# Tanh for sigmoid, Newton steps on GpSimd and a shared key length in the RWKV stage of a macaron block

## The chip, the core and the metric

The kernel runs on one core of a Trainium2 chip. The metric is the device time of one execution in microseconds. A core has engines that work side by side, each through its own queue in order: TensorE (PE; its weight loads are shown as PEld), VectorE (DVE), ScalarE (ACT), GpSimd (POOL), and SyncE (SP), which issues the transfers. Semaphores tie them together: the instruction at a queue's head waits until its inputs and its output buffer are ready, and everything behind it in that queue waits too.

## The reference

Two layers, 512 tokens, 1024 channels, float32 throughout. Each layer is a half feed-forward, a mixing layer and another half feed-forward. The mixing layer joins RWKV-7, gated linear attention and attention over 256 memory rows, each weighted by a sigmoid gate per channel. What the change touches, for 8 RWKV heads of width 64:

```python
v = v + (v_first - v) * jax.nn.sigmoid(v0 + (v @ v1) @ v2)          # second layer only
w_log = -jax.nn.softplus(-(w0 + jnp.tanh(wl) @ w2)) - 0.5           # decay = exp(-exp(w_log))
a = jax.nn.sigmoid(a0 + al @ a2)
kk = kk / jnp.maximum(jnp.linalg.norm(kk, axis=-1, keepdims=True), 1e-12)
k_h = heads(k) * (1.0 + (a_h - 1.0) * k_a)
# per token: state = state * w_t + sa (kk_t * a_t)^T + v_t k_t^T;  y_t = state r_t
yn = (y - mean) * lax.rsqrt(var + RWKV_LN_EPS) * ln_w + ln_b
...
gates = jax.nn.sigmoid(u_gate.reshape(b, s, N_BRANCH, d))
merged = jnp.einsum('bsjc,jcd,bsjd->bsd', branches, w_branch[l], gates)
```

The decay only needs exp(-0.5) * sigmoid(w0 + tanh(wl) w2), so it is a sigmoid too.

## The kernel before

Activations lie with channels on the 128 partitions and 512 tokens along the free axis. Every large product is done three times over, with each float32 operand split into a high part (whi, xhi; L171, an ACT copy) and a low part (wlo, xlo; L172, a DVE subtraction). The weight halves have three buffers each, so ACT and DVE must keep up with TensorE all the time. Line 286 is such a product inside the mixing layer, lines 187 to 189 elsewhere.

The RWKV part is cut into 8 blocks per layer: 4 pairs of heads (hp) times 2 halves of the sequence (hf, 256 tokens, four chunks of 64). A block passes through four generators: `rwkv_gates` (decay, a, the normalized key kk; L359), `rwkv_first` (scaled keys, the chunks' matrices A and Z, the transposed keys KBT), `rwkv_inverse` (inverts the chunk matrices by doubling blocks; X is a 32x32-block transpose of Z by DVE, L510) and `rwkv_second` (the recurrence over chunks; L569 reads the state S, L570 makes qs, L575 applies the inverse, L576 and L577 copy the result into VU, L581 and L587 update S). At its end stands the tail: the product L597, the sums L602 to L607, the square L609 and its sum L611, the deviation L612 to L614, then the transposes L620 on TensorE. Sigmoids for the gates of the branches are in `gate_g`, their use in `branch_g`. Attention heads (L776 to L799) run beside it.

The function `weave` orders TensorE's work by hand. It keeps a clock of planned nanoseconds: each generator yields the TensorE time of its step and how long ACT and DVE will need before its next step, such as

```python
yield 5 * 218, 8500
```

for the tail, to which 400 are added. While no step is due, the order is filled with matmuls of the other branches and projections (L286), one at a time. TensorE's queue keeps exactly this order; if a step's inputs are later than planned, TensorE waits there and all the filling behind it waits too. The order on the other engines comes from a scheduler that places instructions by priority, the block's before the filling's.

ACT evaluates its functions from a table. Where the next function is not in the table that is loaded, an ACT_TABLE_LOAD stands ahead of it in ACT's queue. In the weave Sigmoid, Exp and Sqrt follow each other, in the order the blocks happen to be in.

## Time and profile before

| | us |
|---|---|
| three runs | 2820.02, 2819.43, 2811.11 |
| their median | 2819.43 |
| the profiled execution | 2812.78 |
| its span, first to last instruction | 2811.0 |
| idle time of TensorE, 584 to 940 us (weave, first layer) | 28.2 of 356.0 |
| the same, 1973 to 2332 us (second layer) | 24.3 of 359.0 |
| idle time of TensorE, 1000 to 1795 us (feed-forward) | 0.3 of 795.0 |

A group's row gives the line, the engine, the operation, output and inputs, their shapes, the count, then busy time in us and the mean of one in ns, then the engine's idle time ahead of these instructions and what ended it. A wait's row gives who waited, for whom, and us in total, times and the longest. A matmul's duration (0.39 us for 128x512) includes its way through the array; in a full queue such matmuls follow each other every 0.23 us.

### The profile page before, as it was taken

To read this page: it belongs to the slowest core of one execution; us is meant where nothing else is said; L and a number is where in the kernel's file an instruction comes from. 1 tells how busy PE (TensorE), PEld (TensorE's weight loads), DVE (VectorE), ACT (ScalarE), POOL (GpSimd) and SP (SyncE) were. 2 spreads that over 40 slices of the span, in tenths; PEclk is the share of its full clock that TensorE was granted. 3 is DMA by queue.
4 is the path that set the end of the run, shared out by engine and by line. 5 is a ranking of instruction groups with operands and counts; after the bars stand their busy time and mean duration, and the time that the engine had idled before them with its cause. 6 is when DMAs were issued, how large, how long until landed. Compare 5 with 4: busy or idle time off the path is not lost.

```text
span 2811.0 us, 35290 instructions
## 1 busy us (share of the span) xinstructions
PE 2724.6 (97%) x13296; PEld 2231.9 (79%) x13296; DVE 1636.1 (58%) x3069; ACT 1233.3 (44%) x2097; POOL 21.3 (1%) x118
## 2 busy tenths in 40 slices
PE   8999999998999999999999999999999899999998
PEld 6888887777777888888888888877777788888886
DVE  6434446777877655444454344567788776543444
ACT  5323345665554443333343233465655544432332
POOL 0000000000000000000000000000000000000000
PEclk9999999999999999999999999999999999999999
DMA  5232332211111332222332223312111113322222
GB/s 184 96 100 98 101 135 73 98 58 53 59 64 49 107 118 98 92 103 93 102 105 94 101 98 113 129 68 90 59 59 59 64 63 103 119 98 88 103 93 85
DMA packets 91722, 258.04 MB, mean 92 GB/s; under 512 B 10464, under 2 KB 24832, under 8 KB 91552
## 3 DMA queue, kind: packets, MB, share of 16 engines
q1 hardware_dynamic: 91552, 255.79, 26.5%
q8 instruction: 104, 1.70, 0.2%
q14 instruction: 66, 0.54, 0.1%
HBM read 243.69 MB, written 12.06 MB: 91 GB/s over the span
## 4 chain that ended last, share of the span: by engine, by line
PE 87%; DVE 6%; ACT 5%; issue 1%; DMA 0%; SPq 0%; DVEq 0%; ACTq 0%
PE ps_b L286 20%; PE ps_b L187 19%; PE ps_b L189 19%; PE ps_b L188 19%; PE ps_c L517 2%; PE ps_c L525 1%; PE ps_i L433 1%; DVE t L383 1%; PE ps_f L581 1%; ACT whi L171 1%; ACT L380 1%; PE ps_f L575 0%; PE ps_f L776 0%; PE ps_y L569 0%; PE ps_f L798 0%
## 5 line engine op out<-in xcount | busy, mean ns | idle before, releaser
L171 ACT ACTIVATE whi<-wraw 128x512 fp32r<-128x512 f32 (+1 forms) x874 | 543.3, 622 | 1136.3 <-PE ps_b L188 893.0
L172 DVE TENSOR_TENSOR wlo<-wraw,whi 128x512 fp32r<-128x512 f32 (+1 forms) x874 | 589.2, 676 | 478.0 <-ACT whi L171 474.5
L187 PE MATMUL ps_b<-xhi,whi 128*128 128x512 f32 x1424 | 555.9, 390 | 10.1 <-ACT xhi L197 8.2
L189 PE MATMUL ps_b<-xhi,wlo 128*128 128x512 f32 x1424 | 555.8, 390 | 0.5 <-DVE wlo L172 0.5
L188 PE MATMUL ps_b<-xlo,whi 128*128 128x512 f32 x1424 | 555.8, 390 | 0.0
L286 PE MATMUL ps_b<-xhi,whi 128*128 128x512 f32 x864 | 353.2, 409 | 7.6 <-ACT whi L171 5.8
L286 PE MATMUL ps_b<-xhi,wlo 128*128 128x512 f32 x864 | 350.6, 406 | 3.3 <-DVE wlo L172 3.2
L286 PE MATMUL ps_b<-xlo,whi 128*128 128x512 f32 x864 | 348.7, 404 | 0.0
L187 PEld LDWEIGHTS ps_b<-xhi,whi 128*128 128x128 f32 x1424 | 266.6, 187 | 66.9 <-ACT xhi L197 8.2
L189 PEld LDWEIGHTS ps_b<-xhi,wlo 128*128 128x128 f32 x1424 | 266.6, 187 | 58.1 <-DVE wlo L172 0.9
L188 PEld LDWEIGHTS ps_b<-xlo,whi 128*128 128x128 f32 x1424 | 266.4, 187 | 57.6 <-DVE xlo L198 0.8
L187 PE MATMUL ps_b<-mhi,whi 128*128 128x512 f32 x704 | 277.5, 394 | 0.0
L189 PE MATMUL ps_b<-mhi,wlo 128*128 128x512 f32 x704 | 276.0, 392 | 0.0
L188 PE MATMUL ps_b<-mlo,whi 128*128 128x512 f32 x704 | 273.3, 388 | 0.0
L286 PEld LDWEIGHTS ps_b<-xhi,whi 128*128 128x128 f32 x864 | 164.1, 190 | 45.0 <-ACT whi L171 7.9
L286 PEld LDWEIGHTS ps_b<-xhi,wlo 128*128 128x128 f32 x864 | 163.6, 189 | 39.4 <-DVE wlo L172 6.6
L286 PEld LDWEIGHTS ps_b<-xlo,whi 128*128 128x128 f32 x864 | 164.2, 190 | 30.8 <-issue 1.8
L189 PEld LDWEIGHTS ps_b<-mhi,wlo 128*128 128x128 f32 x704 | 132.1, 188 | 30.9
L188 PEld LDWEIGHTS ps_b<-mlo,whi 128*128 128x128 f32 x704 | 132.2, 188 | 29.5
L187 PEld LDWEIGHTS ps_b<-mhi,whi 128*128 128x128 f32 x704 | 132.4, 188 | 26.3
L262 DVE TENSOR_TENSOR fm<-ps_b,ft 128x512 f32<-128x512 f32 x88 | 60.8, 691 | 127.6 <-PE ps_b L189 127.6
L258 DVE TENSOR_TENSOR ft<-ps_b,rs 128x512 f32<-128x512 f32 x88 | 60.9, 692 | 126.0 <-PE ps_b L189 125.8
(298 smaller groups left out, 3362.9 us busy)
## 6 DMA issues: line engine op xcount, KB each, us to landing
wraw<-in_ffn_in_dram SPq DMA_DIRECT2D x176, 512.0 KB, 3.4
wraw<-in_w_main_dram SPq DMA_DIRECT2D x108, 512.0 KB, 3.4
wraw<-in_ffn_out_dram SPq DMA_DIRECT2D x64, 512.0 KB, 3.4
wraw<-in_ffn_out_dram SPq DMA_DIRECT2D x64, 192.0 KB, 2.3
wraw<-in_w_branch_dram SPq DMA_DIRECT2D x48, 256.0 KB, 2.5
wraw<-in_w_out_dram SPq DMA_DIRECT2D x16, 512.0 KB, 3.4
xd<-x SPq DMA_DIRECT2D x16, 256.0 KB, 2.1
wraw<-in_w_k_dram SPq DMA_DIRECT2D x8, 512.0 KB, 3.6
```

The source lines that it names most:

```text
L171: nc.scalar.activation(hi, r, AF.Copy)
L172: nc.vector.tensor_tensor(lo, r, hi.bitcast(F32), ALU.subtract)
L187: nc.tensor.matmul(ps, a[0], b[0], start=start, stop=False)
L188: nc.tensor.matmul(ps, a[0], b[1], start=False, stop=False)
L189: nc.tensor.matmul(ps, a[1], b[0], start=False, stop=stop)
L258: nc.vector.tensor_tensor(t, pp[0], rs, ALU.mult)
L262: nc.vector.tensor_tensor(m, pp[1], t, ALU.mult)
L286: self.nc.tensor.matmul(ps, w[k][a], xs[k][b], start=k + i == 0, stop=k == n - 1 and i == 2)
L380: nc.scalar.activation(nrm, psn, AF.Sqrt)
L383: nc.vector.reciprocal(rn, nrm)
L433: nc.tensor.matmul(pss[j][:, c * P:(c + 1) * P], KBc[js, c, :], AR[js, c, :], start=True, stop=True)
L517: nc.tensor.matmul(ps[:, u, :], AB[:, u, :], X[:, u, :], start=True, stop=True)
```

## The change

Sigmoids in the weave become tanh: sigmoid(z) is 0.5 tanh(z/2) + 0.5. The halved biases are made once per layer (`half`). For the decay the 0.5 and the sum are one more DVE instruction; elsewhere they go into an instruction that is there already, and the factor two that the branches carry is taken out when the sum is split (scale 0.5). The root of the deviation and its reciprocal become an integer first guess and three Newton steps on GpSimd, 14 dependent instructions on 128x4 values. The key's scaling, square, product with `blk` and root are done once for 512 tokens in a pair's first half. The reciprocal is cut into two of 128 columns. Z's sum with the identity moves ahead, the product KH behind the first steps of the inverse. The copies L539 and L576 go from DVE to ACT. The planner's entry for the tail falls from 8500 to 7500, and those of the gates change with their matmuls.

```diff
+    def hcol(self, name, i):
+        o = (16 if name == "v0" else COLS[name] - COLS["w0"]) + i
+        return self.half[:, o:o + 1]
...
@@ layer_params
+        self.half = self.const.tile([P, 20], F32, name="half", tag="half")
+        for o, name, n in ((0, "w0", 16), (16, "v0", 4)):
+            nc.vector.tensor_scalar(self.half[:, o:o + n], self.par[:, COLS[name]:COLS[name] + n], 0.5, None, ALU.mult)
...
@@ rwkv_rkv
-            nc.scalar.activation(sg, ps, AF.Sigmoid, bias=self.pcol("v0", hp))
+            nc.scalar.activation(sg, ps, AF.Tanh, bias=self.hcol("v0", hp), scale=0.5)
             nc.vector.tensor_tensor(vf, vf, v, ALU.subtract)
-            nc.vector.tensor_tensor(vf, vf, sg, ALU.mult)
-            nc.vector.tensor_tensor(v, v, vf, ALU.add)
+            nc.vector.scalar_tensor_tensor(vf, sg, 1.0, vf, ALU.add, ALU.mult)
+            nc.vector.scalar_tensor_tensor(v, vf, 0.5, v, ALU.mult, ALU.add)
@@ rwkv_gates
-        r, k, v = r[:, cs], k[:, cs], v[:, cs]
-        kk = t1("kk")
-        nc.scalar.activation(kk, k, AF.Copy, scale=self.pcol("k_k", hp))
-        sq = t1("t0", 2)
-        nc.scalar.activation(sq, kk, AF.Square)
-        yield 0, 1300
-
+        if hf == 0:
+
+            self.kk = self.rw.tile([P, T], F32, name="kk", tag="kk", bufs=1)
+            nc.scalar.activation(self.kk, k, AF.Copy, scale=self.pcol("k_k", hp))
+            sq, self.nrm_k = (self.lr.tile([P, T + 1], F32, name=n, tag="ush", bufs=2)[:, :T] for n in ("ksq", "knrm"))
+            nc.scalar.activation(sq, self.kk, AF.Square)
+            yield 0, 1800
+            psn = self.small("i")
+            nc.tensor.matmul(psn, self.c("blk"), sq, start=True, stop=True)
         psw = self.small("i")
...
-        psn = self.small("i")[:, :N]
-        nc.tensor.matmul(psn, self.c("blk"), sq, start=True, stop=True)
         sg, a = t1("sg"), t1("a")
-        nc.scalar.activation(sg, psw[:, :N], AF.Sigmoid, bias=self.pcol("w0", hp))
-        nc.scalar.activation(a, psw[:, N:], AF.Sigmoid, bias=self.pcol("a0", hp))
+        nc.scalar.activation(sg, psw[:, :N], AF.Tanh, bias=self.hcol("w0", hp), scale=0.5)
+        nc.scalar.activation(a, psw[:, N:], AF.Tanh, bias=self.hcol("a0", hp), scale=0.5)
+        if hf == 0:
+            nc.scalar.activation(self.nrm_k, psn, AF.Sqrt)
+        nc.vector.tensor_scalar(sg, sg, 0.5, 0.5, ALU.mult, ALU.add)
         G = t1("G")
         nc.vector.tensor_tensor_scan(G, self.c("reset")[:, :N], sg, 0.0, ALU.mult, ALU.add)
-        nrm = t1("t0", 2)
-        nc.scalar.activation(nrm, psn, AF.Sqrt)
+        r, k, v, kk, nrm = r[:, cs], k[:, cs], v[:, cs], self.kk[:, cs], self.nrm_k[:, cs]
+        kh = t1("t0")
+        nc.vector.tensor_scalar(kh, a, -1.0, self.hcol("k_a", hp), ALU.add, ALU.mult)
+        nc.vector.scalar_tensor_tensor(kh, kh, 1.0, k, ALU.add, ALU.mult)
         nc.vector.tensor_scalar(nrm, nrm, 1e-12, None, ALU.max)
-        rn = t1("t1", 2)
-        nc.vector.reciprocal(rn, nrm)
-        nc.vector.tensor_tensor(kk, kk, rn, ALU.mult)
...
-        nc.vector.tensor_tensor(a, kk, a, ALU.mult)
-        yield 3 * 432, 6500
+        for q in range(2):
+            nc.vector.reciprocal(nrm[:, q * P:(q + 1) * P], nrm[:, q * P:(q + 1) * P])
+        nc.vector.tensor_tensor(kk, kk, nrm, ALU.mult)
+        nc.vector.scalar_tensor_tensor(a, a, 1.0, kk, ALU.add, ALU.mult)
+        yield (2 * 432 if hf else 4 * 432), 6500
@@ rwkv_first
...
-        rk = self.t256("t1", 2)
+        nc.vector.tensor_tensor(Z, A4, self.c("eye").unsqueeze(1).to_broadcast([P, 4, 64]), ALU.add)
+        rk = t1("t1", 2)
         nc.vector.scalar_tensor_tensor(rk, r, self.pcol("r_k", hp), kh, ALU.mult, ALU.mult)
-        KH = rw.tile([P, 4, P], F32, name="KH", tag="KH", bufs=1)
-        nc.vector.tensor_tensor(KH, KBc, E[:, :, 64:65].to_broadcast([P, 4, P]), ALU.mult)
...
-        nc.vector.tensor_tensor(Z, A4, self.c("eye").unsqueeze(1).to_broadcast([P, 4, 64]), ALU.add)
...
         nc.vector.tensor_tensor(z4[:, :, 3:4], z4[:, :, 3:4], t4[:, :, 0:1], ALU.add)
+        KH = rw.tile([P, 4, P], F32, name="KH", tag="KH", bufs=1)
+        nc.vector.tensor_tensor(KH, KBc, E[:, :, 64:65].to_broadcast([P, 4, P]), ALU.mult)
@@ rwkv_inverse
-            nc.vector.tensor_copy(two(W32[96:128])[:, :, f, 32:64], ps[o + 32:o + 64, :, f, :])
+            nc.scalar.activation(two(W32[96:128])[:, :, f, 32:64], ps[o + 32:o + 64, :, f, :], AF.Copy)
@@ rwkv_second
-            nc.vector.tensor_copy(VU[ur, c, 0:64], psu[0:64, 0:64])
+            nc.scalar.activation(VU[ur, c, 0:64], psu[0:64, 0:64], AF.Copy)
...
-        nc.scalar.activation(st, st, AF.Sqrt, bias=self.eps[:, 1:2], scale=1.0 / 64)
-        nc.vector.reciprocal(st, st)
-        nc.vector.tensor_tensor(y4, y4, st.unsqueeze(2).to_broadcast([P, 4, 64]), ALU.mult)
+        nc.gpsimd.tensor_scalar(st, st, 1.0 / 64, LN_EPS, ALU.mult, ALU.add)
+        rt, tt = (rw.tile([P, 4], F32, name=n, tag=n, bufs=1) for n in ("rt", "tt"))
+        nc.gpsimd.tensor_scalar(rt.bitcast(I32), st.bitcast(I32), -0.5, 1597463007.0, ALU.mult, ALU.add)
+        for _ in range(3):
+            nc.gpsimd.tensor_tensor(tt, rt, rt, ALU.mult)
+            nc.gpsimd.tensor_tensor(tt, tt, st, ALU.mult)
+            nc.gpsimd.tensor_scalar(tt, tt, -0.5, 1.5, ALU.mult, ALU.add)
+            nc.gpsimd.tensor_tensor(rt, rt, tt, ALU.mult)
+        nc.vector.tensor_tensor(y4, y4, rt.unsqueeze(2).to_broadcast([P, 4, 64]), ALU.mult)
         self.seconds = 2 * hp + hf + 1
-        yield 5 * 218, 8500
+        yield 5 * 218, 7500
@@ gate_g
-        nc.scalar.activation(s, s, AF.Sigmoid)
+        nc.scalar.activation(s, s, AF.Tanh, scale=0.5)
@@ branch_g
             if first:
-                nc.vector.tensor_tensor(self.x[m], ps, s, ALU.mult)
+                nc.vector.scalar_tensor_tensor(self.x[m], s, 1.0, ps, ALU.add, ALU.mult)
             else:
-                nc.vector.tensor_tensor(s, ps, s, ALU.mult)
+                nc.vector.scalar_tensor_tensor(s, s, 1.0, ps, ALU.add, ALU.mult)
...
```

The built programs show what this does to the order. The instructions named below carry the line numbers of their own program. First ACT's queue in the weave of the first layer, where the gates of the fourth pair's first half (sg, a) meet the tail of an earlier block (the square t of y, and the root st). Before:

```order
L375 ACT_TABLE_LOAD
L375 ACTIVATE sg<-ps_i,par_78 128x256
L612 ACT_TABLE_LOAD
L612 ACTIVATE st<-st,eps 128x4
L376 ACT_TABLE_LOAD
L376 ACTIVATE a<-ps_i,par_78 128x256
L380 ACT_TABLE_LOAD
L380 ACTIVATE t_6819<-ps_i 128x256
L623 ACTIVATE t_6859<-ps_f,par_78 128x256
L398 ACT_TABLE_LOAD
L398 ACTIVATE E<-G 128x4x64
L407 ACTIVATE VU<-ps_i 64x2x128
```

Now, at the same place:

```order
L180 ACTIVATE whi<-wraw 128x512
L387 ACT_TABLE_LOAD
L387 ACTIVATE knrm<-ps_i 128x512
L384 ACT_TABLE_LOAD
L384 ACTIVATE sg<-ps_i,half 128x256
L385 ACTIVATE a<-ps_i,half 128x256
L620 ACTIVATE t_6881<-y 128x256
L180 ACTIVATE whi<-wraw 128x512
L409 ACTIVATE E<-G 128x4x64
L180 ACTIVATE whi<-wraw 128x512
L410 ACTIVATE G<-G 128x256
```

Five table loads within these twelve rows became two, one for the root of the key's length (knrm) and one back; the deviation's root is gone from ACT, and the copies whi stand between the exponentials E and G.

Next DVE's queue at the third block's tail in the first layer, from the sum over the squares to the product that uses the deviation (y). Before:

```order
L611 TENSOR_REDUCE st<-t_6028 128x4
L384 TENSOR_TENSOR kk<-kk,t_6056 128x256
L416 TENSOR_TENSOR AR<-rk_r,E 128x2x2x64
L388 TENSOR_TENSOR a<-kk,a 128x256
L415 SCALAR_TENSOR_TENSOR AR<-kk,E 128x2x128
L458 SCALAR_TENSOR_TENSOR t_6197<-rk_r,par_78,t_6059 128x256
L935 TENSOR_TENSOR gs<-ps_b,rs 128x512
L613 RECIPROCAL st<-st 128x4
L172 TENSOR_TENSOR wlo<-wraw,whi 128x512
L614 TENSOR_TENSOR y<-y,st 128x256
```

Now:

```order
L618 TENSOR_TENSOR y<-y,st 128x256
L622 TENSOR_REDUCE st<-t_6075 128x4
L632 TENSOR_TENSOR y<-y,rt 128x256
L395 TENSOR_SCALAR knrm<-knrm 128x256 x2
L397 RECIPROCAL knrm<-knrm 128x128 x2
L388 TENSOR_SCALAR sg<-sg 128x256
L393 TENSOR_SCALAR t_6151<-a,half 128x256
L390 SCALAR_TENSOR_TENSOR G<-cst,sg 128x256
L394 SCALAR_TENSOR_TENSOR t_6151<-t_6151,rk_k 128x256
L398 TENSOR_TENSOR kk<-kk,knrm 128x256
```

Before, six rows of other work stood between the sum and the deviation's reciprocal and another ahead of the product. Now the product stands right behind the sum, and the key's lengths of the next pair (knrm) and its decay (sg, G) behind the product.

Between those two, GpSimd's queue now holds the chain (shown for the first block of the first layer, down to the end of the first of three equal Newton steps; ush and VU are fills for later work):

```order
L417 MEMSET VU 64x2x128
L624 ISA
L624 TENSOR_SCALAR st<-st 128x4
L312 MEMSET ush 128x1
L626 TENSOR_SCALAR rt<-st 128x4
L628 TENSOR_TENSOR tt<-rt 128x4
L629 TENSOR_TENSOR tt<-tt,st 128x4
L630 TENSOR_SCALAR tt<-tt 128x4
L631 TENSOR_TENSOR rt<-rt,tt 128x4
```

Before, only fills stood in this queue. The row named ISA is there once in the program.

More of the change, by code (lines that the diff above doesn't have):

```diff
@@ L13 @@
 F32R = mybir.dt.float32r
+I32 = mybir.dt.int32
 AF = mybir.ActivationFunctionType
@@ L1011, in mix @@
             self.drain(self.branch_g(0, yh, yl, False, range(8),
-                                     lambda m: self.split(mhi[:, m, :], mlo[:, m, :], self.x[m]), gates))
+                                     lambda m: self.split(mhi[:, m, :], mlo[:, m, :], self.x[m], 0.5), gates))
             for m in range(KD):
```

7 lines of the change are left out of this document (2 added, 5 removed).

## The prediction

> **What bounds the kernel now.** I read four views in this order: the busy line of the page, the stages as windows, TensorE's waits, and a timeline at the worst of them.
>
> ```profile
> PE 2724.6 (97%) x13296; PEld 2231.9 (79%) x13296; DVE 1636.1 (58%) x3069; ACT 1233.3 (44%) x2097; POOL 21.3 (1%) x118
> ```
>
> TensorE is busy for 97% of the span, so the change, which takes nothing from TensorE's arithmetic, can win only where TensorE stands still. The windows show where that is:
>
> ```profile
> 584.00:940.00 356.00, 327.76 (x1945) 270.87 (x1946) 271.81 (x684) 196.20 (x384) 5.38 (x26) 0.99 0.18 61
> 1000.00:1795.00 795.00, 794.73 (x3561) 656.04 (x3560) 381.73 (x584) 285.84 (x458) 1.18 (x6) 1.00 0.30 104
> 1973.00:2332.00 359.00, 334.75 (x1967) 274.65 (x1966) 279.23 (x695) 200.34 (x390) 5.58 (x28) 0.99 0.19 63
> ```
>
> Columns after the width are PE, PEld, DVE, ACT and POOL busy, then the granted clock. The middle row is feed-forward: 0.3 us idle in 795, nothing to win. The other two are the RWKV weave of each layer: 28.2 and 24.3 us idle, 52.5 together. That is about the most the change can take, beside what a lowered clock costs there. DVE is busy 76% of the first weave, ACT 55%. What TensorE waited for over the whole run (us, times, longest):
>
> ```profile
> PE ps_c L517 <- DVE X L510: 8.9, 11, 1.9
> ...
> PE ps_b L286 <- ACT whi L171: 5.8, 2, 3.6
> PE ps_f L620 <- DVE y L614: 5.5, 8, 1.2
> PE ps_y L569 <- DVE S L587: 4.4, 4, 1.6
> PE ps_f L581 <- ACT pr L782: 3.7, 2, 2.0
> PE ps_i L373 <- ACT t L366: 3.7, 1, 3.7
> PE ps_b L286 <- DVE wlo L172: 3.2, 3, 1.4
> PE ps_f L575 <- DVE qs L570: 3.0, 2, 2.0
> ...
> PE ps_f L581 <- ACT VU L577: 2.7, 10, 0.3
> ```
>
> These sum to 40.9 us; the longest single waits, 3.6 and 2.0, are at L286 and L575. The timeline shows both places in layer 0 (the ACT rows, then TensorE's, then the window behind them):
>
> ```profile
> 819.84 1.28 ACT L375 ACT_TABLE_LOAD   x1
> ...
> 823.23 1.28 ACT L376 ACT_TABLE_LOAD   x1
> ...
> 827.18 1.28 ACT L398 ACT_TABLE_LOAD   x1
> ...
> 829.88 1.28 ACT L936 ACT_TABLE_LOAD   x1
> ...
> 832.76 0.61 ACT L171 ACTIVATE whi<-wraw 128x512 fp32r<-128x512 f32 x1
> ```
> ```profile
> 830.56 0.46 PE L575 MATMUL ps_f<-qs,Z 128*128 128x128 f32 x2 [1.99 <-DVE qs L570]
> ...
> 833.43 0.79 PE L286 MATMUL ps_b<-xhi,whi 128*128 128x512 f32 x1 [2.17 <-ACT whi L171]
> ```
> ```profile
> 834.00:838.00 4.00, 4.00 (x11) 2.86 (x10) 2.97 (x6) 0.72 (x2) 0.00 (x0) 0.50 0.51 147
> ```
>
> ACT changes its table six times between 819.8 and 831.2 (four shown), so the next weight half (whi) comes at 832.8 and TensorE stands still twice. Then it runs at half its clock for 4 us (the 0.50), 2 us lost.
>
> **The change, part by part.** Terms in us of the whole program, plus is time won.
>
> *Table loads and copies on ACT.*
>
> ```profile
> L936 ACT ACT_TABLE_LOAD x26 | 33.4, 1283 | 0.5
> L380 ACT ACT_TABLE_LOAD x16 | 20.5, 1283 | 0.3
> L398 ACT ACT_TABLE_LOAD x15 | 19.2, 1283 | 0.3
> L612 ACT ACT_TABLE_LOAD x14 | 18.0, 1283 | 0.2
> ...
> L612 ACT ACTIVATE st<-st,eps 128x4 f32<-128x4 f32 x16 | 4.7, 296 | 0.5 <-DVE st L611 0.4
> ```
> ```profile
> L576 DVE COPY VU<-ps_f 64x64 f32<-64x64 f32 x64 | 13.7, 214 | 5.0 <-PE ps_f L575 3.8
> ...
> L539 DVE COPY w<-ps_c 32x64 f32<-32x64 f32 x32 | 7.2, 225 | 10.0 <-ACT w L538 9.4
> ...
> L613 DVE RECIPROCAL st<-st 128x4 f32<-128x4 f32 x16 | 2.7, 170 | 2.0 <-ACT st L612 2.0
> ```
>
> The built program has 150 table loads before and 76 after: 74 x 1.283 = 95 us fewer, all in or just before the weaves. With the 16 small square roots gone (-4.7) and the 96 copies taken over from DVE (+20.9), ACT sheds about 79 of its 397 us in the two weaves. [...]
>
> Term A, the cluster: the waits of L286 on whi (5.8) and L575 (3.0, DVE itself held up by those loads), plus half clock (2 us, taken the same for layer 1's cluster): 12.8. After the change two loads stand in that place instead of six. I take +12. Bounds: 6.4 (half) and 12.8.
>
> Term B, TensorE's other waits for ACT: 3.7 (pr), 3.7 (t, at the weave's entry) and 2.7 (VU) are 10.1. The entry wait loses the one load in its way, but its square is now 512 wide: +1. Of the other 6.4, which stand behind loads or behind ACT waiting for DVE's half of the same VU copy, two thirds: +4. Both VU copies now run one behind the other on ACT; the second waited for DVE's anyway. B = +5; bounds 0 and 10.
>
> Term C, waits for DVE. It loses 20.9 of copies and 2.7 of reciprocals and gains 16 scalings of the decay's tanh (at L381's 0.29 each, below, 4.7): 19 of 551 us in the weaves. Order counts for more: the 0.68 us product KH now stands behind the inverse's first steps, the sum with the identity is done earlier, and the 1.75 us reciprocal is cut in two, so a wlo need not wait for all of it.
>
> ```profile
> L383 DVE RECIPROCAL t<-t 128x256 f32<-128x256 f32 x16 | 28.0, 1752 | 0.4
> ...
> L460 DVE TENSOR_TENSOR KH<-KB,E 128x512 f32<-128x512 f32 x16 | 10.9, 682 | 0.1
> ...
> L381 DVE TENSOR_SCALAR t<-t 128x256 f32<-128x256 f32 x16 | 4.7, 294 | 5.4 <-ACT t L380 5.3
> ```
>
> Of X 8.9, S 4.4 and wlo 3.2, 16.5 together, I take 40%: +7. Bounds 0 (DVE still sets the pace) and 11. The merge into 512-wide instructions and the doubled gates of the branches replace work of the same size off TensorE's path: 0.
>
> Term D, Newton on GpSimd, the only term that can lose. The tail of each half-head-pair runs 597 (product), 602, sums, 611, deviation, 614, then TensorE's transposes 620. A crowded tail and a quiet one:
>
> ```profile
> 778.77 0.41 DVE L602 TENSOR_TENSOR y<-ps_y,y 64x256 f32<-64x256 f32 x1
> ...
> 783.75 0.41 DVE L611 TENSOR_REDUCE st<-t 128x4 f32<-128x256 f32 x1
> ...
> 788.42 0.41 DVE L614 TENSOR_TENSOR y<-y,st 128x256 f32<-128x256 f32 x1
> ```
> ```profile
> 930.31 0.86 DVE L602 TENSOR_TENSOR y<-ps_y,y 64x256 f32<-64x256 f32 x2 [1.55 <-PE ps_y L597]
> ...
> 933.89 0.42 DVE L611 TENSOR_REDUCE st<-t 128x4 f32<-128x256 f32 x1
> ...
> 936.23 0.42 DVE L614 TENSOR_TENSOR y<-y,st 128x256 f32<-128x256 f32 x1
> ```
>
> Crowded: 10.1 us in all, 4.3 of them from the end of 611 to the start of 614. Quiet: 6.3, of them 1.9. Without the deviation that is 5.8 and 4.4. In its place come 14 dependent GpSimd instructions on 128x4. The trace has only fills there:
>
> ```profile
> L405 POOL MEMSET VU<- 64x256 f32 x16 | 4.9, 307 | 96.3 <-PE ps_y L597 95.9
> ...
> L397 POOL MEMSET E<- 128x4 f32 x16 | 1.7, 106 | 241.8 <-DVE S L587 241.6
> ```
>
> So a step costs between 0.106 (same size, no arithmetic) and 0.307 us (the largest fill of the weave): 1.5 to 4.3 us a chain. I take 0.2, near DVE's 0.170 for 128x4 (L613) plus a hand-over: 2.8 us. Tails become 8.6 and 7.2. The planner now sends the transposes after 7.5 + 0.4 instead of 8.5 + 0.4, so a crowded tail is 0.7 late; sixteen such are 11 us against 5.5 waited at L620 now: D = -6. At 0.106 nothing is late: +5.5. At 0.307 each is 2.2 late: 35 against 5.5, -30. DVE's product with rt waits as well, and the key's reciprocals or weight halves stand behind it in DVE's queue. I cost that at nothing because DVE idles 84 us in the first weave (356.00 - 271.81), ten per tail; without that cover each tail would lose up to the chain's own 2.8 us more. On GpSimd the fills of E, VU and ush stand behind the chain; they are needed a block later. No DMA is added or moved.
>
> Sum: 12 + 5 + 7 - 6 = 18. The profiled execution took 2812.78 us (span 2811.0 and 1.8 around it): 2794.8. The median of the runs shown lies 6.6 higher, where the same gain gives 2801. I forecast **2795**.
>
> **Rivals.** *All waits go* (A 12.8, B 10, C 11, D +5.5 = 39): 2773. For it: ACT sheds a fifth or more of its weave, and one late instruction makes the next late, so relief adds up. Against: DVE stays at three quarters.
>
> *The gain is eaten*: steps of about 0.27 us, 3.8 a chain, tails 1.7 late, 27 - 5.5 = -22 against 24 of the other terms: 2811. No row of the trace excludes this price.
>
> *GpSimd's chain becomes the bound of every tail; slower.* Each step must also read SBUF while DVE streams two SBUF operands (wlo, 0.687 us at 128x512). If it has to wait for such an instruction in half the steps, for half its length, a step costs 0.2 + 0.17 = 0.37, the chain 5.2, a crowded tail 11.0, 3.1 late: 50 - 5.5 = -44, and with the other 24 the time is 2833. It decides above 0.28 us a step, where the losses pass 24. For it: DVE is 76% busy. Against: DVE idles once it has come to its product with rt, and then no one is in the way. [...]
>
> That the change doesn't do what it says (loads stay) is excluded by the 76 in the built program.
>
> **Chances.** Forecast (8.4 to 30 us won) 0.52, all waits go 0.12, eaten 0.18, slower 0.18. About 0.3%, 8.4 us, is what a measurement of this kernel tells from no change. Faster 0.64, same 0.18, slower 0.18. Both signs of D's bound set the range: low 2770 (nearly all waits gone), high 2824 (part of the slow case; the rest, about 0.1, is left out, as is 0.06 below). The forecast's own range is 2783 to 2804.
>
> **What would show each step.** A: two table loads between the gates and the weight halves, no half clock inside a weave. B and C: waits of L581 and X shorter, ACT in a weave near 159 us, DVE near 266. D: the spacing of GpSimd's Newton steps, and the wait before the transposes: 11 us by my price, over 35 in the slow case. Wrong would be a step above 0.28 us, or a weave whose idle time stays though ACT's load has fallen: then DVE alone set the pace.

## The result and the profile after

The changed kernel takes 2841.49 us (median of 7 runs, 2833.48 to 2850.57) against 2820.02 of the kernel before on the same chip: 1.0071 times as long, 95% interval 1.0043 to 1.0098. It is slower by 20 us by this ratio; the forecast was 2795, 18 us less than the profiled execution of the kernel before, and the result lies outside the range. The profiled execution now has a span of 2839.6 us against 2811.0, so 28.6 us are to be found.

The busy line of the page after the change:

```profile
PE 2737.2 (96%) x13280; PEld 2247.1 (79%) x13280; DVE 1617.8 (57%) x2993; ACT 1152.3 (41%) x2079; POOL 72.6 (3%) x342
```

ACT lost 81.0 us of work and DVE 18.3, very nearly what the prediction counted (79 and 19), and still the kernel is slower. TensorE stands idle 102.4 us of the span (2839.6 - 2737.2) against 86.4 before, 16.0 more; and it is busy 12.6 us longer although it has 16 matmuls fewer (the shared key's). These two make up the 28.6. The stages say where (PE, PEld, DVE, ACT and POOL busy, then the granted clock):

```profile
584.00:940.00 356.00, 320.68 (x1854) 268.07 (x1853) 250.28 (x619) 148.87 (x358) 28.11 (x126) 0.94 0.17 56
...
1973.00:2332.00 359.00, 328.10 (x1898) 270.43 (x1896) 264.67 (x631) 159.97 (x370) 29.04 (x131) 0.97 0.17 57
```

In the two weaves the idle time has grown from 28.2 to 35.3 and from 24.3 to 30.9 us although they run on past these windows' ends, and the clock has fallen from 0.99 to 0.94 and 0.97. What TensorE waited for in the weaves over the whole run (us, times, longest; L638 is the old L620, the tail's transposes; L632 the old L614, the product with 1/sqrt; L295 the old L286, L181 the old L172):

```profile
PE ps_f L638 <- DVE y L632: 41.2, 16, 6.1
PE ps_b L295 <- DVE wlo L181: 15.9, 8, 3.6
...
PE ps_i L379 <- ACT ksq L376: 3.9, 1, 3.9
...
PE ps_c L528 <- DVE X L521: 1.2, 4, 0.3
PE ps_f L586 <- DVE qs L581: 0.7, 1, 0.7
```

Of the kinds that summed to 40.9 before, whi at L286, pr at L581 and S at L569 are gone, X fell from 8.9 to 1.2 and qs from 3.0 to 0.7. The wait before the transposes rose from 5.5 to 41.2, in each of the 16 tails, and wlo from 3.2 to 15.9. The first of these is answered one step up, in DVE's waits and in the GpSimd groups of the Newton steps (L624 and L626 once per tail, L628 to L631 three times):

```profile
DVE y L632 <- POOL rt L631: 43.0, 16, 3.9
```
```profile
L628 POOL TENSOR_TENSOR tt<-rt 128x4 f32<-128x4 f32 x48 | 11.8, 246 | 3.8
L631 POOL TENSOR_TENSOR rt<-rt,tt 128x4 f32<-128x4 f32 x48 | 9.8, 205 | 4.0
L629 POOL TENSOR_TENSOR tt<-tt,st 128x4 f32<-128x4 f32 x48 | 9.5, 199 | 3.8
L630 POOL TENSOR_SCALAR tt<-tt 128x4 f32<-128x4 f32 x48 | 9.3, 193 | 4.2
L624 POOL TENSOR_SCALAR st<-st 128x4 f32<-128x4 f32 x16 | 7.7, 484 | 182.3 <-DVE st L622 182.3
...
L626 POOL TENSOR_SCALAR rt<-st 128x4 int32<-128x4 int32 x16 | 3.1, 193 | 1.3
```

Busy time is 51.2 us and the idle time between the steps 17.1 (without the one ahead of L624); together 68.3, or 4.27 us per chain. An undisturbed step is 0.193 to 0.199 us and the next one starts some 0.08 us after its end (17.1 / 208 hand-overs), so 0.28 from start to start. The prediction had 2.8 us per chain.

The half clock shows as a window behind one of these waits. After the change, and then before it for the same stretch of the run:

```profile
708.00:722.00 14.00, 13.20 (x53) 11.96 (x54) 6.22 (x15) 1.79 (x5) 0.40 (x3) 0.51 0.03 9
```
```profile
708.00:722.00 14.00, 13.81 (x94) 11.39 (x94) 10.86 (x31) 6.61 (x14) 0.20 (x1) 1.00 0.20 67
```

```profile
708.80 0.69 PE L638 MATMUL ps_f<-cst,y 128*128 128x128 f32 x2 [2.67 <-DVE y L632]
```

TensorE waited 2.67 us until 708.8, and from 708 to 722 it got half its clock. The wait cost 2.7 us; 14 us at 0.51 of the clock are up to 7 us more. Over the two weaves the clocks of 0.94 and 0.97 are some 32 us of clock not granted (0.06 x 356 + 0.03 x 359); before, with 0.99 in both, it was some 7.

### The profile page after: what moved, and what is told of

Same layout as the page of the kernel before. It is cut to its first block, busy times and chain, and to the rows that moved or that the text cites. A ratio compares the mean times of both kernels' runs of the same rounds, so it can differ in the third digit from the quotient of the medians.

```text
span 2839.6 us, 35473 instructions
## 1 busy us (share of the span) xinstructions
PE 2737.2 (96%) x13280; PEld 2247.1 (79%) x13280; DVE 1617.8 (57%) x2993; ACT 1152.3 (41%) x2079; POOL 72.6 (3%) x342
## 4 chain that ended last, share of the span: by engine, by line
PE 88%; DVE 6%; ACT 2%; POOL 2%; issue 2%; DMA 0%; SPq 0%; DVEq 0%; POOLq 0%; ACTq 0%
PE ps_b L295 21%; PE ps_b L196 19%; PE ps_b L198 19%; PE ps_b L197 18%; PE ps_c L528 2%; PE ps_c L536 1%; DVE wlo L181 1%; PE ps_i L444 1%; PE ps_f L794 1%; PE ps_f L586 1%; PE ps_f L816 1%; DVE knrm L397 0%; POOL tt L628 0%; ACT whi L180 0%; PE ps_y L932 0%
## 5 line engine op out<-in xcount | busy, mean ns | idle before, releaser
L181 DVE TENSOR_TENSOR wlo<-wraw,whi 128x512 fp32r<-128x512 f32 (+1 forms) x874 | 589.9, 676 | 483.7 <-ACT whi L180 475.6
L295 PE MATMUL ps_b<-xhi,wlo 128*128 128x512 f32 x864 | 353.6, 409 | 12.9 <-DVE wlo L181 12.9
L295 PE MATMUL ps_b<-xlo,whi 128*128 128x512 f32 x864 | 355.7, 412 | 0.0
L295 PE MATMUL ps_b<-xhi,whi 128*128 128x512 f32 x864 | 351.1, 406 | 1.8 <-DVE gc L945 1.2
L295 PEld LDWEIGHTS ps_b<-xhi,wlo 128*128 128x128 f32 x864 | 165.7, 192 | 48.0 <-DVE wlo L181 15.9
L295 PEld LDWEIGHTS ps_b<-xhi,whi 128*128 128x128 f32 x864 | 165.6, 192 | 40.1 <-issue 5.6
L295 PEld LDWEIGHTS ps_b<-xlo,whi 128*128 128x128 f32 x864 | 165.8, 192 | 31.6 <-issue 1.8
L198 PEld LDWEIGHTS ps_b<-mhi,wlo 128*128 128x128 f32 x704 | 132.1, 188 | 30.9
```

Of the source, the lines that this page charges most:

```text
L181: nc.vector.tensor_tensor(lo, r, hi.bitcast(F32), ALU.subtract)
L198: nc.tensor.matmul(ps, a[1], b[0], start=False, stop=stop)
L295: self.nc.tensor.matmul(ps, w[k][a], xs[k][b], start=k + i == 0, stop=k == n - 1 and i == 2)
```

## The experiments

Each kernel was timed beside the kernel before on the same chip; the ratio is to that one. In the short names "square root" means ScalarE's Sqrt and DVE's reciprocal in the deviation, as before the change, and "entry" the planner's number behind the tail. Waits are those of TensorE before the transposes, the clock is the mean granted one; both are of the profiled execution. Microseconds given behind a difference of two ratios are that difference times 2820.

| version | median us | ratio | 95% interval | waits, us | clock |
|---|---|---|---|---|---|
| the change: Newton, entry 7500 | 2841.5 | 1.0071 | 1.0043 to 1.0098 | 41.2 | 0.985 |
| square root, entry 8500 (e1) | 2794.4 | 0.9917 | 0.9885 to 0.9949 | 5.4 | 0.992 |
| square root, entry 7500 (e7) | 2803.5 | 0.9939 | 0.9920 to 0.9957 | 13.0 | 0.989 |
| Newton, entry 8500 (e13) | 2812.6 | 0.9969 | 0.9953 to 0.9985 | 13.7 | 0.991 |
| Newton, entry 10500 (e2) | 2826.4 | 1.0027 | 1.0008 to 1.0045 | 0.8 | 0.988 |

**Newton taken out.** The first question was whether the rest of the change (tanh, key, copies, order) does what the prediction said.

```diff
-        nc.gpsimd.tensor_scalar(st, st, 1.0 / 64, LN_EPS, ALU.mult, ALU.add)
...
-        nc.vector.tensor_tensor(y4, y4, rt.unsqueeze(2).to_broadcast([P, 4, 64]), ALU.mult)
+        nc.scalar.activation(st, st, AF.Sqrt, bias=self.eps[:, 1:2], scale=1.0 / 64)
+        nc.vector.reciprocal(st, st)
+        nc.vector.tensor_tensor(y4, y4, st.unsqueeze(2).to_broadcast([P, 4, 64]), ALU.mult)
...
-        yield 5 * 218, 7500
+        yield 5 * 218, 8500
```

> The change, but the deviation is ACT's square root and DVE's reciprocal again, and the planner's entry for the tail 8500 as before; all else stays. Theory 1 (the chain of 14 GpSimd instructions costs the time: 43 us of DVE held, 41 us of TensorE waiting before the transposes, and the half clock that these long waits bring): the waits before the transposes fall to about 6 us, the half clock in the weaves to that of before or less, and the time to 2785 to 2805, though each tail brings its table loads back. Theory 3 (another part of the change, such as the key's length taken for 512 tokens or both VU copies on ACT, costs it): still 2830 or more.

2794.44 us, ratio 0.9917 [0.9885, 0.9949]: 23 us faster than the kernel before, within the range that theory 1 gave. TensorE's waits, of this version:

```profile
PE ps_b L295 <- DVE wlo L181: 16.1, 8, 3.6
...
PE ps_f L632 <- DVE y L626: 5.4, 4, 2.1
PE ps_f L586 <- DVE qs L581: 4.6, 4, 1.9
```

The wait before the transposes is back at 5.4, so the whole loss lies in the chain and its entry. The waits for wlo stay at 16.1: they do not come from Newton. (This version has 104 table loads, 28 more than the change, because of the 16 roots, so it is a little less than A, B and C were meant to give.)

**Newton alone.** The mirror image: the kernel before, with the 14 GpSimd instructions in the place of square root and reciprocal, entry 8500, nothing else of the change.

```diff
-        nc.scalar.activation(st, st, AF.Sqrt, bias=self.eps[:, 1:2], scale=1.0 / 64)
-        nc.vector.reciprocal(st, st)
+        nc.gpsimd.tensor_scalar(st, st, 1.0 / 64, LN_EPS, ALU.mult, ALU.add)
...
```

> The kernel before with one part of the change, Newton's steps on GpSimd in place of ACT's root and DVE's reciprocal; the planner's entry stays 8500. Theory 1: tails are 1 us or more late, the waits before the transposes rise from 5.5 to 20 us or more, the half clock in the weaves grows, and the time is 2825 to 2845. Theory 2 (allowance alone) and theory 3: within 0.3% of before, or faster by ACT's 14 loads.

2833.80 us, ratio 1.0053 [1.0032, 1.0074]: 15 us slower.

```profile
PE ps_f L627 <- DVE y L621: 15.1, 15, 2.2
```

The chain loses by itself, without the rest of the change. The time is in the range of theory 1, the wait is not: it rose from 5.5 to 15.1 where 20 or more were expected. The profiled spans differ by 23.1 us; 8.2 of them are idle time of TensorE and 14.9 are busy time (2739.5 us against 2724.6 for the same matmuls, at a mean clock of 0.989 against 0.994).

**More room in the plan.** The change with an entry of 10500.

```diff
-        yield 5 * 218, 7500
+        yield 5 * 218, 10500
```

> The change, but the planner's entry for the tail is 10500 instead of 7500. Theory 1: the chain still takes 4.3 us and still holds DVE for some 40 us, so waits for wlo stay (about 16 us), but TensorE is sent to the transposes 3 us later, and most of its 41 us of waiting there goes: 2800 to 2820. Theory 2 (only the planner's allowance is wrong, the chain itself costs nothing): waits before the transposes and for wlo both go, full clock, 2790 or less. Theory 3: 2830 or more.

2826.37 us, ratio 1.0027 [1.0008, 1.0045]. Of the waits before the transposes 0.8 us are left, but the kernel is still slower than before, and slower than the 2800 to 2820 that theory 1 gave; it had left the waits for wlo at 16 us:

```profile
PE ps_b L295 <- DVE wlo L181: 37.8, 8, 7.4
```
```profile
DVE y L632 <- POOL rt L631: 40.4, 14, 3.8
```

DVE still stands 40 us at its product, and the weight halves stand behind the product in DVE's queue. In the longest waits for wlo DVE comes from a wait of 2.6 or 3.7 us at the product and then works almost without a break up to the weight half (at the gates of the first layer from 837.5 to 848.1). With the transposes out of the way, TensorE waits up to 7.4 us at once for those. Part of the 37.8 may come from the late entry itself and not from the chain: no run has the square root at 10500, and with 9500 it waits 21.3 us for wlo (below).

**The same steps on DVE.** All 14 instructions on VectorE in place of GpSimd, entry 7500.

```diff
-        nc.gpsimd.tensor_scalar(st, st, 1.0 / 64, LN_EPS, ALU.mult, ALU.add)
+        nc.vector.tensor_scalar(st, st, 1.0 / 64, LN_EPS, ALU.mult, ALU.add)
...
```

> The change, but the same 14 instructions run on DVE instead of GpSimd (planner's entry 7500). Theory 1: a step on DVE costs 0.17 us or less instead of 0.28 and no other engine holds DVE, so the chain takes about 2.5 us, a tail is late by 0 to 1 us, and the time is 2790 to 2815 although DVE gets 37 us more work. Theory 3: 2840 or more, DVE being busier.

2854.89 us, ratio 1.0128 [1.0099, 1.0157], the slowest of all. Theory 1 (2790 to 2815) fell, and the time is one that theory 3 gave, DVE being busier.

```profile
PE ps_f L638 <- DVE y L632: 54.2, 14, 8.3
```
```profile
702.62 0.16 DVE L624 TENSOR_SCALAR st<-st 128x4 f32<-128x4 f32 x1
702.70 0.68 DVE L531 TENSOR_TENSOR W<-ps_c,cst 128x512 f32<-128x512 f32 x1
...
705.57 0.16 DVE L631 TENSOR_TENSOR rt<-rt,tt 128x4 f32<-128x4 f32 x1
705.76 0.16 DVE L628 TENSOR_TENSOR tt<-rt 128x4 f32<-128x4 f32 x1
...
707.35 0.42 DVE L632 TENSOR_TENSOR y<-y,rt 128x256 f32<-128x256 f32 x1
```

A step is 0.2 us from start to start there, less than GpSimd's 0.28, but the chain of 4.7 us (702.62 to 707.35) has other work between its first steps. Over the 16 tails it is 5.1 us from the first step to the product, against 4.4 on GpSimd in the change. DVE's load did not show where weight halves are waited for (wlo 9.0 us against 15.9 in the change); it shows inside the chain. So the crossing to GpSimd is not needed for the loss; that the number of steps makes it is what the next two runs show.

**Fewer steps.** Two Newton steps (10 instructions), as the diff has it, and one (6), both at the change's entry. They leave out one and two of the three steps, so the deviation is less exact.

```diff
-        for _ in range(3):
+        for _ in range(2):
```

> The change with two Newton steps in place of three: 10 GpSimd instructions a tail in place of 14, all else the same (1/sqrt is then a little less exact; this leaves out the third step). Theory 1 (the length of the chain sets the loss): 4 instructions at 0.278 us are 1.1 us less per tail, so TensorE's waits before the transposes (41.2 us with three steps) fall by up to 16 x 1.1 = 18 us, to some 23 to 30, half clock falls with them by a third of the 27 us it cost more, and the time is 2841 - 14 to 18 - 9 = 2814 to 2820. Theory 2 (it is the crossing to GpSimd and back and the order of DVE's queue that cost, whatever the chain's length): the waits stay at 36 to 41 us and the time at 2833 or more.

> The change with one Newton step: 6 GpSimd instructions a tail (this leaves out two of the three steps, so that the deviation is only approximate). Theory 1 (length of the chain): 8 instructions at 0.278 us are 2.2 us less per tail; the chain is then about 2 us, as long as the square root and reciprocal that stood there; waits before the transposes 5 to 12 us, half clock about as in the version with the square root, time 2795 to 2805. Theory 2 (crossing and queue order): waits 30 us or more, time 2828 or more. Between the two, a straight line through three, two and one steps would say what a step costs the kernel.

2821.74 us (1.0004 [0.9988, 1.0019]) and 2809.18 us (0.9966 [0.9946, 0.9986]). TensorE's wait with two steps, and then with one:

```profile
PE ps_f L638 <- DVE y L632: 22.3, 12, 4.5
```
```profile
PE ps_f L638 <- DVE y L632: 8.6, 6, 3.1
```

41.2, 22.3, 8.6: each Newton step less (four instructions of 0.278 us) takes 1.1 us off each tail, 17.8 us off sixteen, and TensorE's wait falls by 18.9 and then by 13.7, as long as tails are late at all. In time a Newton step was worth 0.0067 and 0.0038 of the ratio, 19 and 11 us. The length of the chain is the cause; the second theory, that the crossing alone costs, falls with 8.6 us left. Both came out a little slower than expected (2814 to 2820 and 2795 to 2805).

**The entry.** The square root with the change's entry, as the diff has it, and with a later one (9500).

```diff
-        yield 5 * 218, 8500
+        yield 5 * 218, 7500
```

> The version with ScalarE's square root in the deviation, but with the change's planner entry of 7500 in place of 8500. Theory 1 (in the change the entry lost a little, the chain the most): each of 16 tails is asked for 1 us earlier, so waits before the transposes rise from 5.4 to at most 5.4 + 16 = 21 us, likely 10 to 14, and the time from 2794 to 2799 to 2806. Rival (the entry is what lost; the Newton chain would have been hidden with the old entry): waits before the transposes 30 us or more, time 2820 or more. Third: the entry does nothing, 2794 within 0.2%.

> The version with ScalarE's square root and a planner's entry of 9500 in place of 8500. The entries 7500 and 8500 gave 2804 and 2794 with 13.0 and 5.4 us of waits before the transposes. Theory 1 (an entry is good as long as waits before the transposes shrink; later, the transposes come where they hold up the waits elsewhere): the waits before the transposes fall to 0 to 3 us, those for wlo rise from 16 to 20 or more as they did with 10500 and the Newton steps, and the time is 2793 to 2803. Rival (a later entry is free): 2785 to 2791.

2803.54 us (0.9939 [0.9920, 0.9957]) and 2807.55 us (0.9955 [0.9936, 0.9975]), against 2794 at 8500. With 7500 the wait before the transposes is 13.0 us in place of 5.4; with 9500 it is gone, and these stand in the list:

```profile
PE ps_b L295 <- DVE wlo L181: 21.3, 8, 4.7
...
PE ps_c L528 <- DVE X L521: 6.2, 6, 3.1
```

8500 lies between two losses: earlier, the transposes wait; later, wlo and X are waited for. Why a later entry brings those waits was not followed up. 9500 came out beyond the range that was expected (2793 to 2803). Between 7500 and 8500 the two intervals overlap, so the time alone does not settle that the entry costs the square root version anything; the waits do.

**The chain with nobody waiting for it.** The square root version, with the 14 GpSimd instructions run beside it on the sums and their result unused.

```diff
+        nc.scalar.activation(sd, st, AF.Sqrt, bias=self.eps[:, 1:2], scale=1.0 / 64)
+        nc.gpsimd.tensor_scalar(ev, st, 1.0 / 64, LN_EPS, ALU.mult, ALU.add)
...
+        nc.vector.reciprocal(sd, sd)
+        nc.vector.tensor_tensor(y4, y4, sd.unsqueeze(2).to_broadcast([P, 4, 64]), ALU.mult)
```

> The version with ScalarE's square root, and beside it the 14 GpSimd instructions of the Newton chain run on a copy of the sums; nobody uses what they give (added work, the computation is whole). Theory 1 (the chain costs because the product waits for it, not because GpSimd works beside VectorE): the time is 2794 within 0.2%, waits before the transposes 4 to 8 us. [...]

2795.02 us, ratio 0.9908 [0.9883, 0.9932]: the time of the version without them. The busy lines of the two, without the chain and with it:

```profile
PE 2720.7 (97%) x13280; PEld 2235.6 (80%) x13280; DVE 1619.5 (58%) x3009; ACT 1191.7 (43%) x2123; POOL 21.5 (1%) x118
```
```profile
PE 2723.3 (97%) x13280; PEld 2237.7 (80%) x13280; DVE 1619.5 (58%) x3009; ACT 1191.7 (43%) x2123; POOL 74.8 (3%) x342
```

GpSimd worked 53 us more and DVE's busy time is the same to the tenth. What the change loses, it loses by waiting for the chain; work on GpSimd beside DVE did not slow DVE.

**The parts that win.** Three versions take one part each out of the square root version. The key's length per half of 256 tokens:

```diff
-        if hf == 0:
-            self.kk = self.rw.tile([P, T], F32, name="kk", tag="kk", bufs=1)
...
+        r, k, v = r[:, cs], k[:, cs], v[:, cs]
+        kk = t1("kk")
+        nc.scalar.activation(kk, k, AF.Copy, scale=self.pcol("k_k", hp))
...
+        nc.vector.reciprocal(rn, nrm)
```

> The version with ScalarE's square root, and the key's length worked out per half of 256 tokens again (two squares, two products, two square roots and two 256-wide reciprocals per pair of heads, as before the change; tanh and the copies on ScalarE stay). Theory 1 (the key's work for both halves in one burst on DVE is what makes wlo late: TensorE waits 16.1 us for wlo with it, 3.2 in the kernel before): the waits for wlo fall to 3 to 6 us, some half clock goes with them, time 2775 to 2788. Rival (wlo waits come from the tanh and copies, that is from the order of ScalarE's work): wlo stays at 12 to 18 us, and the time is 2794 to 2802 for the 8 more square roots with their tables and the longer reciprocals.

The copies on VectorE again:

```diff
-            nc.scalar.activation(two(W32[96:128])[:, :, f, 32:64], ps[o + 32:o + 64, :, f, :], AF.Copy)
+            nc.vector.tensor_copy(two(W32[96:128])[:, :, f, 32:64], ps[o + 32:o + 64, :, f, :])
...
-            nc.scalar.activation(VU[ur, c, 0:64], psu[0:64, 0:64], AF.Copy)
+            nc.vector.tensor_copy(VU[ur, c, 0:64], psu[0:64, 0:64])
```

> The version with ScalarE's square root in the deviation, and the 96 small copies (VU's upper half, the inverse's lower block) on VectorE again. What it loses against 2794 is the worth of the copies. Theory 1 (VectorE's load sets the weave's pace beside ScalarE's clusters; my term C): 20.9 us of copies on VectorE bring back waits of the X and VU kind, and the time is 2800 to 2806. Rival (the copies were off the path on either engine): 2791 to 2798, waits for X within 3 us of those with the copies on ScalarE. Third: ScalarE, freed of them, has its weight halves ready earlier, and the time falls below 2790.

The sigmoids back:

```diff
-        nc.scalar.activation(sg, psw[:, :N], AF.Tanh, bias=self.hcol("w0", hp), scale=0.5)
-        nc.scalar.activation(a, psw[:, N:], AF.Tanh, bias=self.hcol("a0", hp), scale=0.5)
+        nc.scalar.activation(sg, psw[:, :N], AF.Sigmoid, bias=self.pcol("w0", hp))
+        nc.scalar.activation(a, psw[:, N:], AF.Sigmoid, bias=self.pcol("a0", hp))
...
-        nc.scalar.activation(s, s, AF.Tanh, scale=0.5)
+        nc.scalar.activation(s, s, AF.Sigmoid)
```

> The version with ScalarE's square root, and sigmoids again in place of tanh (the doublings that go with it undone too; key per pair and copies on ScalarE stay). What it loses against 2794 is the worth of the tanh. Theory 1 (my term A: the cluster of table loads ahead of a weight half was what TensorE waited for): some 50 table loads come back, waits for whi of 4 to 8 us return with half clock, and the time is 2804 to 2812. Rival (the cluster went with the merged key, which had half of its square roots, not with the tanh): waits for whi stay under 3 us and the time is 2792 to 2799.

They took 2806.60 us (0.9950 [0.9929, 0.9972]), 2803.67 (0.9938 [0.9918, 0.9959]) and 2803.20 (0.9939 [0.9918, 0.9960]). Beside 2795.0 (0.9908) of the same version with the unused chain, which ran on the chip of the last two, each part is worth something like 8 us (the first about 9 by its ratio to 0.9917); the intervals of the ratios overlap, so the parts are not ranked. The key per half missed both ranges (2775 to 2788 and 2794 to 2802), so undoing the shared key was wrongly expected to gain; the copies met the time of theory 1 but not its waits for X and VU; the sigmoids lie between the two ranges, with the waits for whi of theory 1 but without its half clock (0.992 as with the tanh). TensorE's waits that tell them apart, with the key per half and then with the sigmoids:

```profile
PE ps_c L527 <- DVE X L520: 11.2, 11, 2.5
PE ps_b L295 <- DVE wlo L181: 9.2, 6, 2.5
...
PE ps_y L579 <- DVE S L597: 4.6, 2, 2.4
PE ps_f L591 <- ACT pr L793: 3.5, 2, 1.7
```
```profile
PE ps_b L295 <- DVE wlo L181: 10.1, 5, 3.6
...
PE ps_b L295 <- ACT whi L180: 5.4, 2, 2.7
PE ps_f L803 <- DVE pr L797: 3.9, 1, 3.9
```

With the sigmoids back the whi waits return (5.4 against 5.8 before the change), and with them 144 table loads where the square root version has 104: the cluster of loads was the tanh's to remove. But the place still waits. At the gates, where the kernel before and the sigmoid version wait for whi, the square root version waits for wlo (2.86 us at 834.7 and 1.63 at 2222.2, part of its 16.1), so that of these waits little was gained, and the tanh's worth is in smaller waits such as pr (3.9). With the key per half, X, S and pr return, so these went with the shared key. The waits for wlo fall from 16.1 to 9.2, not to the 3 to 6 expected. The longest two, 3.56 us in each layer, are not there any more (the longest left is 2.51); they stood behind DVE's work on the key, here in the first layer (DVE, then TensorE):

```profile
678.25 0.68 DVE L494 TENSOR_TENSOR KH<-KB,E 128x512 f32<-128x512 f32 x1
678.85 1.76 DVE L397 RECIPROCAL knrm<-knrm 128x128 f32<-128x128 f32 x2
680.52 0.63 DVE L181 TENSOR_TENSOR wlo<-wraw,whi 128x512 fp32r<-128x512 f32 x1
```
```profile
681.21 0.80 PE L295 MATMUL ps_b<-xhi,wlo 128*128 128x512 f32 x1 [3.56 <-DVE wlo L181]
```

The shared key wins all the same. The product KH, whose place the change also moved, stands shortly ahead of the weight half in all six waits for wlo in the weaves of the square root version; no run moved it back, so its share is open. With the copies on DVE the wlo waits were 20.5 us in place of 16.1 and X stayed small: the copies help by freeing DVE for the weight halves.

Waits are not all of it. With the copies on DVE TensorE's idle time is 2.7 us longer than in the square root version and its busy time 8.5, with the key per half 2.3 and 9.2, with the sigmoids 6.2 and 1.5. In these executions the first two parts pay mainly through the clock (0.988 in both against 0.992).

**Chain and entry together.** The change with only its entry put back.

```diff
-        yield 5 * 218, 7500
+        yield 5 * 218, 8500
```

> The change with its planner's entry put back from 7500 to 8500; the three Newton steps on GpSimd stay. With the square root the entry 7500 cost 9 us against 8500 (2803.5 and 2794.4). Theory 1 (the chain is the loss; the entry adds its 1 us per tail on top of it): waits before the transposes fall from 41 to 25 to 32 us and the time from 2841 to 2822 to 2832, so still some 30 us above the square root at the same entry. Rival (the entry is most of the loss): waits before the transposes under 12 us, time under 2812.

2812.56 us, ratio 0.9969 [0.9953, 0.9985]: just beyond the rival's numbers and far from those of theory 1. One number of the plan turned the sign of the change.

```profile
PE ps_b L295 <- DVE wlo L181: 23.8, 10, 7.3
PE ps_f L638 <- DVE y L632: 13.7, 10, 2.9
```

The Newton chain costs 0.0052 (15 us) with the entry 8500, the same as in the kernel before (0.0053), but 0.0132 (37 us) with 7500. The entry alone costs 0.0022 (6 us, not clear of noise) with the square root and 0.0102 (29 us) with Newton. Chain and entry 7500 together cost 0.0154, twice the sum of 0.0052 and 0.0022. A tail that is in time by 1 us loses nothing when it becomes 1 us longer; with both, all 16 are late (16 waits, against 10, 10 and 4 in the other three).

The mean granted clocks say the rest. The executions of one kernel differ mostly by the clock: the kernel before took spans from 2808 to 2828 us at clocks from 0.995 down to 0.987, but span times clock was 2791 to 2796 in all of them. For Newton at 7500, Newton at 8500, the square root at 7500 and the square root at 8500 this product is 2797, 2786, 2773 and 2769 us (medians of all executions), and what is left of the span, the clock not granted, is 43, 25, 29 and 22. So the chain costs 17 us of the product at 8500 and 24 at 7500, and with 7500 it loses 13 us of clock besides. By the same product the key per half costs 3 us, the copies on DVE 2 and the sigmoids 6 (2772, 2771 and 2776 against 2769).

## Why the prediction was wrong

**The sum of A, B and C (24) was about right, its terms were not.** With Newton out of the way the gain is 23 us by the ratio, 19.2 between the profiled executions. That the sum came out is in part luck. A: the cluster of loads is gone and whi's waits with it, as argued. In the changed kernel two loads stand ahead of the weight halves at the gates, as forecast:

```profile
837.68 1.28 ACT L387 ACT_TABLE_LOAD   x1 [2.10 <-PE ps_i L379]
...
839.59 1.28 ACT L384 ACT_TABLE_LOAD   x1
...
841.92 0.63 ACT L180 ACTIVATE whi<-wraw 128x512 fp32r<-128x512 f32 x1
```

But of A's 5.8 us at L286 only 1.3 were won in the square root version, because TensorE waits 4.5 there for wlo in place of whi, and the qs waits rose from 3.0 to 4.6. "No half clock inside a weave" did not come either: in the square root version the clock is 0.97 from 584 to 700 us and 0.91 from 830 to 850, and behind the waits that end at 681.21 and 834.69 (3.56 and 2.86 us) matmuls of 128x512 follow each other every 0.43 us in place of 0.23, for some 3 us. The kernel before was at half clock in two places of its weaves, from 831.7 to 838.5 and from 2224.3 to 2231.1, 6.8 us each and not the 4 that the prediction read from a window. Its two weaves have a mean clock of 0.99, and those of the square root version have 0.99 too, so A's 4 us for it were not won. B won more than its 5: pr and VU at L581 are gone (6.4). C won 11.2 of X and S and lost 12.9 of wlo (4.5 of them at A's place), so less than nothing in sum where +7 was taken; "so a wlo need not wait for all of it" was wrong. In the rows shown with the key's experiment a wlo does stand behind both cut reciprocals. The rest of the gain came from small waits that the prediction had not listed and from the merge, costed at nothing and worth about as much as the tanh. (A slip in the reading: the prediction calls 3.6 and 2.0 the longest single waits, but its own list has 3.7 at L373.)

**Term D (-6) was the step that failed**, in three places.

- *The price of a step.* 0.2 us was taken, near DVE's 0.170 for the same size plus a hand-over. It measured 0.278: 0.195 of work and 0.08 of hand-over. The bound of 0.307, from the largest fill, would have been nearer. As a sign of being wrong a step above 0.28 was named; at 0.278 that sign would not have spoken.
- *The length of the chain.* 4.27 us in place of 2.8. Of it, 0.44 are steps held up while DVE reads (last section). In the first chain there is a wait besides: a fill of ush stands between its first two steps in GpSimd's queue and waits 1.7 us for TensorE. By the prediction's own rule a crowded tail is then 5.8 + 4.3 = 10.1 us against its place of 7.9, 2.2 late, 35 us in sixteen; measured 41.2. The sixteen tails of the change, from L613 (the old L602) to the end of the product, last 8.6 to 11.9 us, 10.2 in the mean. At entry 8500 the rule gives 1.2 late, 19 us; measured 13.7. The rule was good; the price was not. That alone would have moved the sum from +18 to -6 (24 - 30), which is 2819, no change within the 0.3% that the prediction names.
- *A term that was missing.* The prediction took half clock as something that A removes. It grew with the waits instead: against the square root version, TensorE's waits before the transposes are 35.8 us longer and TensorE is busy 16.5 us longer with the same work (2737.2 and 2720.7). These 52.3, less the 3.9 us that qs is shorter, are 48.4; the spans differ by 47.8. That half clock follows long waits is seen in these sums and in single places of the traces; which wait brings it is open (last section).

**The rivals.** Slower by GpSimd's chain was the right sign with 0.18, but for only part of its reason: it wanted half of the steps held up by DVE and 0.37 us each. No run shows that term of 0.17 us a step: 14 of the 224 steps were held up, by 7 us in all or 0.03 a step. The price of a step was that of the rival *eaten* (0.27, chain 3.8). That rival came to 2811 because its chain was 0.5 us shorter than the measured one and because it had no half clock in it, as the "decides above 0.28 us a step" had none; with half clock the balance tips at a lower price.

**The cover.** DVE's wait at the product was costed at nothing, since DVE idles ten us per tail. DVE did wait 43.0 us there. In the change itself the cover held as far as weight halves go: wlo is waited for 15.9 us, and 16.1 with the square root. With entry 10500 it fails, with 37.8 us of waits for wlo. That is 21.7 more than with the square root at 8500, about half of the 45 us that the prediction put as the most that sixteen tails could lose without cover.

## What to carry to other kernels

Price a chain of small dependent instructions by steps times start-to-start time (0.28 us on GpSimd, 0.20 on DVE here, for 128x4), not by busy time, add what other work can get between the steps, and set the sum against the slack of the place where it stands: here 14 steps could not replace two instructions, though they free ACT of a table load. A plan's due time and the length of what it waits for are one number; change one and the other must follow, and a forecast has to add them before it asks which tails are late. Where waits grow, add what a lowered clock takes behind them. Here that was 16.5 us of busy time for 35.8 of waits between the change and the square root, and 14.9 for 9.6 with Newton alone, so it is a range and not a factor.

## What the runs showed of the hardware

**GpSimd's read held up by DVE.** A chain at the crowded gates, GpSimd first and then DVE's queue at that time:

```profile
844.57 1.71 POOL L624 TENSOR_SCALAR st<-st 128x4 f32<-128x4 f32 x1 [7.33 <-DVE st L622]
846.36 0.19 POOL L626 TENSOR_SCALAR rt<-st 128x4 int32<-128x4 int32 x1
```
```profile
844.39 0.42 DVE L399 SCALAR_TENSOR_TENSOR a<-a,kk 128x256 f32<-128x256 f32 x1
...
845.80 0.42 DVE L432 SCALAR_TENSOR_TENSOR KB<-a,G 128x256 f32<-128x256 f32 x1
849.93 0.42 DVE L632 TENSOR_TENSOR y<-y,rt 128x256 f32<-128x256 f32 x1 [3.71 <-POOL rt L631]
```

An instruction of 0.19 us took 1.71 and ended 0.06 us after the last of a run of DVE instructions (six in the trace from 844.39 on, of which the first and last are shown) that each read two operands in SBUF; the next one took 0.19 again. The 14 steps that took 0.49 us or more all look like this: each ended 0.05 to 0.07 us after a DVE instruction with two operands in SBUF. Steps beside a DVE instruction that reads PSUM were not longer (L626 at 704.74 took 0.19 while L531 read ps_c from 704.52 to 705.20). The rival made too much of it: once DVE stands at the product, nothing is in the way, as the prediction itself had put against it. Over all chains the hold-up is 7 us: the sixteen L624 are 4.7 us above undisturbed steps in sum, the forty-eight L628 2.3. The other direction, DVE held up by GpSimd, was not seen (1619.5 us of DVE with and without the chain).

**Half clock behind a wait.** In the stretch with 0.51 above, the clock fell at 708.1, 2.0 us into the wait of 2.67 us, and stayed at half until 721.8. In the 4 us before, TensorE was busy for 2.14, at the full clock:

```profile
704.00:708.00 4.00, 2.14 (x12) 1.49 (x10) 1.89 (x4) 0.76 (x2) 2.84 (x13) 1.00 0.26 66
```

Not every wait did it. This one in the same weave was longer, and the window around it has the full clock:

```profile
672.19 0.41 PE L638 MATMUL ps_f<-cst,y 128*128 128x128 f32 x2 [3.53 <-DVE y L632]
```
```profile
666.00:676.00 10.00, 6.47 (x30) 4.85 (x29) 5.68 (x13) 6.71 (x10) 2.81 (x15) 1.00 0.13 42
```

What decides between the two was not settled, and so a forecast can add half clock behind long waits only as a share.
